# A hybrid encoder layer on one core: the residual's gate moved among the gate paths, and the rows of the first keys and queries kept in the probabilities' buffers

## The chip, the cores and the metric

The kernel runs on one core of a Trainium2 chip. The metric is the device time of one execution in microseconds (us); lower is better. The engines are TensorE (PE, matmuls; PEld are its weight loads), VectorE (DVE), ScalarE (ACT), GpSimd (POOL), and SyncE (SP), whose queue issues nearly all DMAs.

## What is computed

One encoder layer is applied to two requests (prompt and sample), each 1024 tokens of 1024 channels, with shared weights, in float32. Cut to what matters:

```python
mod = silu(c) @ w_ada + b_ada
shift, scale, gate = split(mod, 3)                 # gate: the residual's gate
h = rms_norm(x, norm_g) * (1 + scale) + shift
qa, ka, va, za, qb, kb, vb, zb, ga, gb = split(h @ w_in, ...)
qa, ka = rope_axial(rms_norm(qa, qn_a)), rope_axial(rms_norm(ka, kn_a))   # 8 and 2 heads of 64
oa = gqa_attention(qa, ka, va) * silu(za)
qb, kb = rope(rms_norm(qb, qn_b)), rope(rms_norm(kb, kn_b))               # 4 heads, two maps each
ob = rms_norm(softmax(q1 k1) v - lam * softmax(q2 k2) v, subln_g) * (1 - lam_init) * silu(zb)
merged = sigmoid(ga) * (oa @ w_proj_a) + sigmoid(gb) * (ob @ w_proj_b)
y = x + gate * (merged @ w_out)
```

## The kernel before

Everything is float32 in, float32 out. Most matmuls are split: a weight or an activation is kept as a high part (a copy in float32r, by ScalarE) and a low part (the difference, by VectorE), and a product is three matmuls. `load_w` loads 256 columns of a weight in four pieces through three small staging buffers (`st`, line 229), splits each piece (lines 203, 204) and puts the parts into one of two weight buffers (`wpool`, tag `w`, 16 KB per partition). These two buffers are shared by all weights.

The kernel is written as Python generators. Each `yield` is a step, and `weave` (line 80) draws steps from several streams in turns: each stream has a number of steps that it is thought to have and a lead, and the one that is least far along goes next. So the order in which instructions are written down comes from constants at the top of the file. A planner then fixes the order of each engine's queue at build time, from modelled durations, with the written order as priority; the attention's instructions get a higher one (line 976). On the chip every queue, TensorE's and SP's among them, runs in its fixed order and waits where it must.

One request goes like this.

- **Head** (`head`, line 1114): keys and values of branch A (`kva_gen`) and the first half of its queries (`qa_gen`). `pipelined` makes a tile of 128 tokens by `proj_tt` (a product of 24 matmuls, line 596), then a *front* (copy, squares and their sum, a power for the inverse norm, rotation: `rows`, lines 604 to 615, and `rope`, 617 to 638; on VectorE and GpSimd by turns) that leaves a finished row tile, and up to `LAG` tiles later a *back*: one or two transpositions on TensorE (line 649) and the split into keys or queries (651, 652). A row tile is one of three buffers (`rtile`, line 175).
- For the first request, products of the first four token tiles are summed while the modulation is still being made (`sums_early`); they sit in the four banks that the scores use later (`early`). So for tiles 0 to 3 `proj_tt` has nothing to do and returns the sum given.
- **Gate paths** (`z_gen`, line 786): 12 items (`z_item`) of 256 columns for `za`, `zb`, `ga`, `gb`, each of 12 steps of 8 matmuls (line 797). The result is stored to DRAM (line 784). The stream `zs` chains the 12 items, and every phase takes some of its steps: a phase takes three times its number in `Z_SHARE` (the fourth and the fifth are heads 1 and 2; the sixth isn't used).
- **Attention** (`attention`, line 959): first branch A in two halves (phases 0 and 1), then four heads of branch B (phases 2, 3, 4 and the last). A score tile is four matmuls (824, 825), a maximum (826), an exponential (828), and, once two maps are joined (860), a transposition within blocks by VectorE (861) and four DMAs (`flip`, 866) that turn the probabilities; the values follow (886, 887 for A, 926 for B). Probabilities lie in four buffers of 128 x 1024 (`ptile`, line 160).
- Beside the phases the other projections are made: the second half of the queries in phase 0, values and queries and keys of B in phase 1 and so on.
- **Last phase** (line 1256): the last head's attention, woven with `fill()` and `gates()`. `gates` multiplies branch outputs by their gates (`gated_gen`: rows are loaded again, 1028 to 1036, and split, 1043). `fill` is: what is left of `zs`, then, for the first request, `gate_gen()`, then the merges (`merge_gen`, 1070).
- After it the rest of the merges, the output projection (`out_gen`, line 1101) and, beside it, the second request's normalised input (`ht_gen`).

`gate_gen` (line 516) makes the residual's gate for both requests: four groups of 256 columns of `w_ada`. For each group, four loads of 256 KB through the staging buffers (line 525), eight matmuls (two pieces of the profile each) that put four strips of the sum into four quarters of a bank (line 528), a copy (534), two small matmuls that add the strips (537), the bias and a factor (539, 542). It yields eight times.

Of the kernel before, what the change touches and what calls it, by code (L numbers as in the profile page):

```python
# [12 lines left out]
F32 = mybir.dt.float32  # L13
F32R = mybir.dt.float32r
AF = mybir.ActivationFunctionType
ALU = mybir.AluOpType
# [18 lines left out]


Z_SHARE = (
    (8, 19, 6, 3, 3, 3),
    (13, 12, 7, 3, 0, 6),
)  # L40
Z_HEAD = (8, 6)
Z_HEAD_A = (-0.3, -0.12)
ATT_W = (
    (0.944, 1.018, 1.232, 1.187, 1.03, 1.769),
    (1.017, 1.209, 1.063, 1.196, 0.764, 1.069),
)
IN_A = (
    (0.1, -0.05, 0.7, 0.05, 0.2, 0.15),
    (0.1, -0.05, 0.43, 0.3, 0.15, 0.55),
)  # L50
Z_A = (
    (0.25, 0.05, 0.3, -0.05, -0.1, 0.0),
    (0.05, 0.05, 0.35, 0.15, -0.3, -0.2),
)
LAST_ATT = (47, 45)
LAST_FILL = (21, 25)
GATED_A = (0.1, 0.1)
LATE_A = 1.0
QUARTER_P = 200
KV_STEPS = 12  # L60
QA_A = 0.0
FIRST_ATT = 16
FIRST_A = 0.18
Z_SPLIT = 6
TAIL = (2, 5)
TAIL_A = (1.15, 1.15)
LAG = 2
Z_FIRST = (7, 10)
Z_FIRST_A = (0.0, 0.0)

CUTS = (3, 6)

# [7 lines left out]
def weave(*streams):  # L80

    live = [[g, n, 0, ahead] for g, n, ahead in streams if n > 0]
    while live:
        s = min(live, key=lambda s: s[2] / s[1] - s[3])
        if next(s[0], None) is not None:
            s[2] += 1
        else:
            live.remove(s)


def drain(*gens):
    for g in gens:
        if g is not None:
            for _ in g:
                pass
# [13 lines left out]
def kernel(ctx: ExitStack, tc: tile.TileContext, t: dict):  # L109
# [19 lines left out]
    def nm(s):  # L129
        uid[0] += 1  # L130
        return f"{s}_{uid[0]}"
# [8 lines left out]
    def gbank():  # L140
        turn[0] += 1
        if alone[0] and not early and turn[0] % 5 in (0, 2):
            return sbank()[:, :512]
        return fbank()
# [24 lines left out]
    def halves2(pt):  # L169
        return pt[:, :512], pt[:, 512:]  # L170
# [4 lines left out]
    def rtile():  # L175
        return mtile("row", [P, 512], bufs=3)
# [337 lines left out]


    def gate_gen():
        for n in range(4):
            acc = gbank()[:, :256]
            nc.vector.memset(acc, 0.0)
            for q in range(2):  # L520
                sts = []
                for i in range(2):
                    st = spool.tile([P, 2, 256], F32, tag="st", name=nm("st"))
                    row, col = q * 512 + i * 256, 2 * D + n * 256
                    dma(st, w_ada[row : row + 256, col : col + 256].rearrange("(c p) n -> p c n", p=P))
                    sts.append(st)
                for c in (2, 3, 0, 1):
                    nc.tensor.matmul(
                        acc[32 * c : 32 * c + 2], cT[:, q * 4 + c], sts[c // 2][:, c % 2], start=(q == 0), stop=(q == 1),
                        tile_position=(0, 32 * c),  # L530
                    )
                yield 1
            part = rtile()[:, :256]
            nc.vector.tensor_copy(part, acc)
            ps = gbank()[:, :4].rearrange("p (c g) -> p c g", g=2)
            for c in range(2):
                nc.tensor.matmul(ps[:, c, :], part[:, c * P : (c + 1) * P], two, start=True, stop=True)
            cs = slice(n * 2, n * 2 + 2)
            nc.vector.tensor_tensor(
                out=gatec[:, cs], in0=ps, in1=bcol[:, 2, cs].unsqueeze(2).to_broadcast([P, 2, 2]), op=ALU.add  # L540
            )
            nc.vector.tensor_scalar(out=gatec[:, cs], in0=gatec[:, cs], scalar1=0.5, scalar2=None, op0=ALU.mult)

    def ht_gen(g, ht):
        ss = const.tile([P, NTT], F32, name="ssx")
# [54 lines left out]
    def by_turns(tt):  # L600

        return nc.vector if alone[0] and tt % 2 == 0 else nc.gpsimd

    def rows(ps, nh, rs):

        n = nh * HD
        row = rtile()
        raw, sq = row[:, :n], row[:, 256 : 256 + n]
        nc.scalar.activation(raw, ps, AF.Copy)
        nc.scalar.activation(sq, raw, AF.Square, scale=1.0 / math.sqrt(HD))  # L610
        ss = tiny.tile([P, 4], F32, tag="ss", name=nm("ss"))[:, :nh]
        nc.vector.tensor_reduce(out=ss, in_=sq.rearrange("p (h d) -> p h d", d=HD), axis=AX.X, op=ALU.add)
        nc.vector.tensor_scalar(out=ss, in0=ss, scalar1=EPS, scalar2=None, op0=ALU.add)
        nc.gpsimd.tensor_tensor(out=rs, in0=ss, in1=nhalf[:, :nh], op=ALU.pow)
        return (x.rearrange("p (h d) -> p h d", d=HD) for x in (raw, sq))
# [38 lines left out]
    def pipelined(ht, w, front, back, given={}, rest=0):  # L654
        pend = []
        for tt in range(NTT):
            ps = yield from proj_tt(ht, w, tt, given)
            pend.append((tt, front(tt, ps)))
            if len(pend) > LAG:
                back(*pend.pop(0))  # L660
            if tt + 1 == rest:
                while pend:
                    back(*pend.pop(0))
            yield 1
        while pend:
            for _ in range(1 if alone[0] else 3):
                yield 1
            back(*pend.pop(0))
        yield 1
# [444 lines left out]
    def head(g, st, zs, late):  # L1114
        kva, qa = kva_gen(st["ht"], st), qa_gen(st, 0)

        def folded():
            by_q(st["cosA"], st["sinA"], gqa, 16)
            st["turned"] = True

        nz = 3 * Z_HEAD[g]
        if g == 0:
            rs = late[0]()
            weave((islice(zs, 6), 6, 0.0), (late[1](rs), 4, LATE_A))
            weave((kva, 27, 0.0), (islice(zs, Z_FIRST[0]), Z_FIRST[0], Z_FIRST_A[0]))
            drain(islice(qa, KV_STEPS))
            early.clear()
            folded()
        else:
            weave((kva, 27, 0.0), (islice(zs, Z_SPLIT), Z_SPLIT, Z_HEAD_A[0]))  # L1130
            folded()
            weave((qa, 27, 0.0), (islice(zs, nz - Z_SPLIT), nz - Z_SPLIT, Z_HEAD_A[1]))
        return qa

    def new_state(g):
# [55 lines left out]
    def z_item(st, i):  # L1191
        ht = st["ht"]
        if i < 2:
            w = kva_w[2][0] if i == 0 and st is states[0] else None
            return z_gen(ht, C_ZA + i * 256, st["zd"], i * 2, True, w)
        if i < 4:
            return z_gen(ht, C_ZB + (i - 2) * 256, st["zd"], i * 2, True)
        i -= 4
        if i % 2 == 0:
            return z_gen(ht, C_GA + i * 128, st["gad"], i, False)  # L1200
        return z_gen(ht, C_GB + (i - 1) * 128, st["gbd"], i - 1, False)
# [4 lines left out]
    for g in range(2):  # L1206
        st = states[g]
        ht = st["ht"]
        load_tables_A(st)
        zs = chain(*[z_item(st, i) for i in range(12)])  # L1210
        qa = head(g, st, zs, late)
        alone[0] = False
        if g == 0:
# [32 lines left out]

        def fill():
            yield from zs
            if g == 0:
                yield from gate_gen()  # L1250
            drain(first)
            yield from islice(merge, 16 - TAIL[g])

# [64 lines left out]
```

## Time and profile before

| | |
|---|---|
| runs | 1953.32, 1954.51, 1960.04 us; median 1954.51 |
| the profiled execution | 1953.03 us, span 1951.2 us, mean granted clock 0.982 |
| TensorE busy | 1865.0 us (96%) |
| weight loads (PEld) | 1609.4 us (82%) |
| VectorE busy | 1398.9 us (72%) |
| ScalarE, GpSimd busy | 994.9 us (51%), 412.1 us (21%) |
| DMA | 299.48 MB, mean 153 GB/s |

A row of waits reads "engine, tile, line, waited for engine, tile, line: us in total, times, longest". A row of a time line reads "start, duration, engine, line, operation, output <- input, shapes, count [idle before it <- what ended the idle]". A row of windows gives a stretch, its length, the busy time of PE, PEld, DVE, ACT and POOL with their counts of instructions, the mean granted TensorE clock, the share of the DMA engines' time and GB/s. SPq is SyncE's queue. The last attention phase of the first request runs from about 755 to 860 us; its first merge (line 1070) starts at 838.56 us.

### The profile page before, as it was taken

How to read it: one execution, taken by the hardware profiler on the slowest of the kernel's cores; microseconds unless marked ns; L12 is line 12 of the kernel's file. 1: busy time of each engine (PE TensorE's matmuls, PEld its weight loads, DVE VectorE, ACT ScalarE, POOL GpSimd, SP SyncE). 2: the span in 40 equal slices, each digit the busy share in tenths (PEclk: the TensorE clock that was granted, in tenths of full speed). 3: DMA queues.
4: the chain of work that ended last, by engine and by line, in shares of the span. 5: the costliest groups of instructions: out<-in, count | busy, mean ns of one | idle time of the engine just before them, and what ended most of it. 6: DMA issues, size and time to landing. Idle time of an engine off the chain costs nothing.

```text
span 1951.2 us, 30752 instructions
## 1 busy us (share of the span) xinstructions
PE 1865.0 (96%) x10406; PEld 1609.4 (82%) x10406; DVE 1398.9 (72%) x2160; ACT 994.9 (51%) x2095; POOL 412.1 (21%) x766
## 2 busy tenths in 40 slices
PE   6879999999999999699999999999999999999999
PEld 4768888888888898477889888888888899778887
DVE  4667986778887667767475688767878876887731
ACT  3546765666665545422333466656667555643310
POOL 0252310032424233000023322001322332410000
PEclk9989999999999999799999999999999999999999
DMA  9125555556554435887552355656565443578632
GB/s 322 47 70 149 150 158 140 156 146 153 153 145 120 104 96 141 251 281 216 200 182 63 107 133 139 186 130 169 143 160 148 129 131 99 129 239 260 216 103 76
DMA packets 280316, 299.48 MB, mean 153 GB/s; under 512 B 38304, under 2 KB 233056, under 8 KB 280160
## 3 DMA queue, kind: packets, MB, share of 16 engines
q1 hardware_dynamic: 280160, 297.51, 54.1%
q8 instruction: 84, 1.38, 0.3%
q14 instruction: 72, 0.59, 0.1%
HBM read 137.91 MB, written 42.04 MB: 92 GB/s over the span
## 4 chain that ended last, share of the span: by engine, by line
PE 58%; DVE 14%; DMA 11%; SPq 7%; issue 4%; ACT 4%; POOL 2%; ACTq 0%; DVEq 0%; POOLq 0%
PE f L596 13%; PE f L797 12%; PE f L1070 6%; DMA q<-p 6%; PE f L1101 6%; SPq L866 5%; PE a L926 4%; PE s L1101 3%; PE s L824 3%; PE s L825 3%; DVE m L826 3%; DVE q L875 3%; DVE p L861 2%; PE s L1070 2%; ACT p L828 1%
## 5 line engine op out<-in xcount | busy, mean ns | idle before, releaser
L797 PE MATMUL f<-u,w 128*128 128x512 f32 x2136 | 547.1, 394 | 4.5 <-DVE w L204 2.3
L596 PE MATMUL f<-w,u 128*128 128x256 f32 x3264 | 456.0, 285 | 0.7 <-DVE u L652 0.5
L797 PEld LDWEIGHTS f<-u,w 128*128 128x128 f32 x2136 | 387.8, 188 | 79.7 <-DVE w L204 3.5
L596 PEld LDWEIGHTS f<-w,u 128*128 128x128 f32 x3264 | 428.9, 191 | 18.2 <-DVE u L652 0.9
L826 DVE TENSOR_REDUCE m<-s 128x1 f32<-128x1024 f32 x256 | 310.9, 1218 | 42.5 <-PE s L825 39.5
L861 DVE STREAM_TRANSPOSE p<-p 128x1024 f32<-128x1024 f32 x192 | 238.3, 1241 | 105.0 <-ACT p L828 103.7
L825 PE MATMUL s<-u,sw 128*128 128x512 f32 x512 | 207.0, 405 | 0.9 <-DMA sw<-u 0.9
L875 DVE TENSOR_TENSOR q<-q,hi 128x512 fp32r<-128x512 f32 x256 | 173.0, 692 | 37.5 <-ACT hi L874 34.7
L828 ACT ACTIVATE p<-s,m,rsA 128x1024 f32<-128x1024 f32 x128 | 154.0, 1203 | 86.9 <-DMA q<-p 79.4
L874 ACT ACTIVATE hi<-q 128x512 fp32r<-128x512 f32 x256 | 152.9, 624 | 74.5 <-DMA q<-p 40.0
L828 ACT ACTIVATE p<-s,m,rsB 128x1024 f32<-128x1024 f32 x128 | 154.4, 1206 | 14.8 <-DMA q<-p 7.2
L203 ACT ACTIVATE w<-st 128x512 fp32r<-128x512 f32 x188 | 109.3, 625 | 99.2 <-PE f L1101 34.3
L204 DVE TENSOR_TENSOR w<-st,w 128x512 fp32r<-128x512 f32 x188 | 126.3, 703 | 32.9 <-ACT w L203 32.2
L1070 PE MATMUL f<-u,w 128*128 128x512 f32 x576 | 140.0, 395 | 0.6 <-DVE u L1043 0.5
L886 PE MATMUL a<-hi,u 128*128 128x256 f32 x512 | 133.0, 285 | 3.9 <-DVE oo L903 3.3
L887 PE MATMUL a<-q,u 128*128 128x256 f32 x512 | 131.0, 288 | 2.2 <-DVE q L875 2.2
L926 PE MATMUL a<-q,u 128*128 128x256 f32 x512 | 125.2, 386 | 4.9 <-DVE w L204 2.5
L1070 PEld LDWEIGHTS f<-u,w 128*128 128x128 f32 x576 | 108.7, 190 | 24.8 <-DVE u L1043 0.9
L742 POOL TENSOR_TENSOR row<-row,gB 128x96 f32<-128x96 f32 x64 | 30.0, 470 | 445.2 <-ACT row L610 445.2
L824 PE MATMUL s<-u 128*128 128x512 f32 x256 | 111.8, 437 | 9.6 <-ACT p L828 9.6
L825 PEld LDWEIGHTS s<-u,sw 128*128 128x128 f32 x512 | 99.5, 194 | 17.6 <-issue 1.1
L926 PEld LDWEIGHTS a<-q,u 128*128 128x128 f32 x512 | 96.1, 194 | 21.8 <-issue 5.6
(184 smaller groups left out, 2623.5 us busy)
## 6 DMA issues: line engine op xcount, KB each, us to landing
q<-p SPq DMA_DIRECT2D x768, 128.0 KB, 2.7
st<-in_w_in_dram SPq DMA_DIRECT2D x128, 256.0 KB, 3.2
zd<-ev SPq DMA_DIRECT2D x96, 256.0 KB, 2.2
sw<-u SPq DMA_DIRECT2D x256, 64.0 KB, 2.1
p<-zd SPq DMA_DIRECT2D x64, 256.0 KB, 3.6
u<-in_w_ada_dram SPq DMA_DIRECT2D x16, 512.0 KB, 8.8
st<-in_w_in_dram SPq DMA_DIRECT2D x64, 128.0 KB, 3.1
st<-in_w_out_dram SPq DMA_DIRECT2D x32, 256.0 KB, 3.9
```

What stands on the lines that cost most here:

```text
L596: nc.tensor.matmul(ps, lt[c][:, sl], w[c][:, wi, :], start=(k == 0), stop=(k == 23))
L797: nc.tensor.matmul(ps, w[c][:, wi, e * P : (e + 1) * P], rt[c], start=(k == 0), stop=(k == 23),)
L824: nc.tensor.matmul(s[:, sl], q, k[:, sl], start=True, stop=False)
L825: nc.tensor.matmul(s[:, sl], sw, k[:, sl], start=False, stop=True)
L826: nc.vector.tensor_reduce(out=m, in_=s, axis=AX.X, op=ALU.max, negate=True)
L828: nc.scalar.activation(pt.rearrange("p (j c a) -> p j c a", j=4, c=8), s.rearrange("p (c a j) -> p j c a", c=8, j=4), AF.Exp, scale=rs, bi ...
L861: nc.vector.transpose(pt, pt)
L874: nc.scalar.activation(th, tl.bitcast(F32), AF.Copy)
L875: nc.vector.tensor_tensor(out=tl, in0=tl.bitcast(F32), in1=th.bitcast(F32), op=ALU.subtract)
L926: nc.tensor.matmul(acc, u["v"][:, k], pT[:, k], start=(k == 0), stop=(k == 7))
L1070: nc.tensor.matmul(ps, w[:, c, wi, d * P : (d + 1) * P], o[:, oi, :], start=(k == 0), stop=(k == 11))
L1101: nc.tensor.matmul(ps, w[c][:, wi, e * P : (e + 1) * P], m[:, mi, :], start=(k == 0), stop=(k == 23))
```

## The change

- `gate_gen` no longer runs in `fill` between the last gate path and the merges. It stands in the chain `zs` of the first request behind item 9 (`GATE_AT`), as eight steps among the gate paths' steps.
- It loads 512 columns of `w_ada` at a time, in four DMAs of 512 KB, into one of the two weight buffers, twice; the staging buffers aren't used. The matmuls are the same in number and shape.
- In the first request's head the fronts of the four given tiles of keys, and then those of queries, are written down first (12 steps each), with their row tiles in halves of the probabilities' buffers (`row_early`). `pipelined` does no back while tiles are given, and yields once before the queries' four backs. Then come the rest of the keys, woven with 9 steps of the gate paths (7 before), and the queries' backs.
- In the second request's head keys and queries are one stream, woven with 18 steps of the gate paths that start later.
- Constants: steps per phase, leads, the rates of the attention in the phases, the rates in the last phase.

```diff
@@ -35,38 +35,37 @@
 
 
 Z_SHARE = (
-    (8, 19, 6, 3, 3, 3),
+    (8, 21, 4, 2, 4, 3),
     (13, 12, 7, 3, 0, 6),
 )
 Z_HEAD = (8, 6)
-Z_HEAD_A = (-0.3, -0.12)
+Z_HEAD_A = (-0.3, -0.32)
 ATT_W = (
-    (0.944, 1.018, 1.232, 1.187, 1.03, 1.769),
-    (1.017, 1.209, 1.063, 1.196, 0.764, 1.069),
+    (0.944, 1.067, 1.232, 1.093, 1.03, 1.769),
+    (1.017, 1.367, 1.063, 1.196, 0.764, 1.069),
 )
 IN_A = (
-    (0.1, -0.05, 0.7, 0.05, 0.2, 0.15),
+    (0.1, -0.07, 0.7, 0.05, 0.25, 0.15),
     (0.1, -0.05, 0.43, 0.3, 0.15, 0.55),
 )
 Z_A = (
-    (0.25, 0.05, 0.3, -0.05, -0.1, 0.0),
-    (0.05, 0.05, 0.35, 0.15, -0.3, -0.2),
+    (0.25, 0.05, 0.2, -0.05, -0.1, 0.0),
+    (0.03, 0.05, 0.35, 0.15, -0.3, -0.2),
 )
-LAST_ATT = (47, 45)
-LAST_FILL = (21, 25)
+LAST_ATT = (47, 43)
+LAST_FILL = (22, 23)
 GATED_A = (0.1, 0.1)
 LATE_A = 1.0
 QUARTER_P = 200
 KV_STEPS = 12
-QA_A = 0.0
-FIRST_ATT = 16
-FIRST_A = 0.18
-Z_SPLIT = 6
+GATE_AT = 9
+FIRST_ATT = 15
+FIRST_A = 0.16
 TAIL = (2, 5)
 TAIL_A = (1.15, 1.15)
 LAG = 2
-Z_FIRST = (7, 10)
-Z_FIRST_A = (0.0, 0.0)
+Z_FIRST = (9, 8)
+Z_FIRST_A = (-0.05, 0.0)
 
 CUTS = (3, 6)
 
@@ -514,32 +513,35 @@
 
 
     def gate_gen():
-        for n in range(4):
-            acc = gbank()[:, :256]
-            nc.vector.memset(acc, 0.0)
-            for q in range(2):
-                sts = []
-                for i in range(2):
-                    st = spool.tile([P, 2, 256], F32, tag="st", name=nm("st"))
-                    row, col = q * 512 + i * 256, 2 * D + n * 256
-                    dma(st, w_ada[row : row + 256, col : col + 256].rearrange("(c p) n -> p c n", p=P))
-                    sts.append(st)
-                for c in (2, 3, 0, 1):
-                    nc.tensor.matmul(
-                        acc[32 * c : 32 * c + 2], cT[:, q * 4 + c], sts[c // 2][:, c % 2], start=(q == 0), stop=(q == 1),
-                        tile_position=(0, 32 * c),
-                    )
-                yield 1
-            part = rtile()[:, :256]
-            nc.vector.tensor_copy(part, acc)
-            ps = gbank()[:, :4].rearrange("p (c g) -> p c g", g=2)
-            for c in range(2):
-                nc.tensor.matmul(ps[:, c, :], part[:, c * P : (c + 1) * P], two, start=True, stop=True)
-            cs = slice(n * 2, n * 2 + 2)
-            nc.vector.tensor_tensor(
-                out=gatec[:, cs], in0=ps, in1=bcol[:, 2, cs].unsqueeze(2).to_broadcast([P, 2, 2]), op=ALU.add
-            )
-            nc.vector.tensor_scalar(out=gatec[:, cs], in0=gatec[:, cs], scalar1=0.5, scalar2=None, op0=ALU.mult)
+        for half in range(2):
+            w = wpool.tile([P, NCH, 512], F32, tag="w", name=nm("wg"))
+            for q in range(4):
+                row, col = q * 256, 2 * D + half * 512
+                dma(
+                    w[:, q * 2 : q * 2 + 2],
+                    w_ada[row : row + 256, col : col + 512].rearrange("(c p) n -> p c n", p=P),
+                )
+            for n in (half * 2, half * 2 + 1):
+                cols = slice(n % 2 * 256, n % 2 * 256 + 256)
+                acc = gbank()[:, :256]
+                nc.vector.memset(acc, 0.0)
+                for q in range(2):
+                    for c in range(4):
+                        nc.tensor.matmul(
+                            acc[32 * c : 32 * c + 2], cT[:, q * 4 + c], w[:, q * 4 + c, cols], start=(q == 0),
+                            stop=(q == 1), tile_position=(0, 32 * c),
+                        )
+                    yield 1
+                part = rtile()[:, :256]
+                nc.vector.tensor_copy(part, acc)
+                ps = gbank()[:, :4].rearrange("p (c g) -> p c g", g=2)
+                for c in range(2):
+                    nc.tensor.matmul(ps[:, c, :], part[:, c * P : (c + 1) * P], two, start=True, stop=True)
+                cs = slice(n * 2, n * 2 + 2)
+                nc.vector.tensor_tensor(
+                    out=gatec[:, cs], in0=ps, in1=bcol[:, 2, cs].unsqueeze(2).to_broadcast([P, 2, 2]), op=ALU.add
+                )
+                nc.vector.tensor_scalar(out=gatec[:, cs], in0=gatec[:, cs], scalar1=0.5, scalar2=None, op0=ALU.mult)
 
     def ht_gen(g, ht):
         ss = const.tile([P, NTT], F32, name="ssx")
@@ -601,10 +603,17 @@
 
         return nc.vector if alone[0] and tt % 2 == 0 else nc.gpsimd
 
+    spare, held = [], [False]
+
+    def row_early():
+        if not spare:
+            spare.extend(halves2(ptile()))
+        return spare.pop(0)
+
     def rows(ps, nh, rs):
 
         n = nh * HD
-        row = rtile()
+        row = row_early() if held[0] else rtile()
         raw, sq = row[:, :n], row[:, 256 : 256 + n]
         nc.scalar.activation(raw, ps, AF.Copy)
         nc.scalar.activation(sq, raw, AF.Square, scale=1.0 / math.sqrt(HD))
@@ -656,9 +665,10 @@
         for tt in range(NTT):
             ps = yield from proj_tt(ht, w, tt, given)
             pend.append((tt, front(tt, ps)))
-            if len(pend) > LAG:
+            while len(pend) > LAG and tt >= len(given):
                 back(*pend.pop(0))
             if tt + 1 == rest:
+                yield 1
                 while pend:
                     back(*pend.pop(0))
             yield 1
@@ -1117,19 +1127,21 @@
         def folded():
             by_q(st["cosA"], st["sinA"], gqa, 16)
             st["turned"] = True
+            yield from ()
 
         nz = 3 * Z_HEAD[g]
         if g == 0:
             rs = late[0]()
             weave((islice(zs, 6), 6, 0.0), (late[1](rs), 4, LATE_A))
-            weave((kva, 27, 0.0), (islice(zs, Z_FIRST[0]), Z_FIRST[0], Z_FIRST_A[0]))
-            drain(islice(qa, KV_STEPS))
+            held[0] = True
+            drain(islice(kva, 12), islice(qa, 12))
+            held[0] = False
+            weave((kva, 15, 0.0), (islice(zs, Z_FIRST[0]), Z_FIRST[0], Z_FIRST_A[0]))
+            next(qa)
             early.clear()
-            folded()
+            drain(folded())
         else:
-            weave((kva, 27, 0.0), (islice(zs, Z_SPLIT), Z_SPLIT, Z_HEAD_A[0]))
-            folded()
-            weave((qa, 27, 0.0), (islice(zs, nz - Z_SPLIT), nz - Z_SPLIT, Z_HEAD_A[1]))
+            weave((chain(kva, folded(), qa), 52, 0.0), (islice(zs, nz), nz, Z_HEAD_A[g]))
         return qa
 
     def new_state(g):
@@ -1207,7 +1219,7 @@
         st = states[g]
         ht = st["ht"]
         load_tables_A(st)
-        zs = chain(*[z_item(st, i) for i in range(12)])
+        zs = chain(*[x for i in range(12) for x in (z_item(st, i), gate_gen())[: 1 + (i == GATE_AT and g == 0)]])
         qa = head(g, st, zs, late)
         alone[0] = False
         if g == 0:
@@ -1246,8 +1258,6 @@
 
         def fill():
             yield from zs
-            if g == 0:
-                yield from gate_gen()
             drain(first)
             yield from islice(merge, 16 - TAIL[g])
```

## The prediction

> **What bounds the kernel now.** First the page: the shares of the engines and the slices.
>
> ```profile
> span 1951.2 us, 30752 instructions
> PE 1865.0 (96%) x10406; PEld 1609.4 (82%) x10406; DVE 1398.9 (72%) x2160; ACT 994.9 (51%) x2095; POOL 412.1 (21%) x766
> PE   6879999999999999699999999999999999999999
> PEclk9989999999999999799999999999999999999999
> ```
>
> TensorE is the bound: 86.2 us of the span without a matmul (1951.2 - 1865.0). A schedule change can win only those and the time in which the granted clock was below 1. Both lie in two places, the first three slices and the one slice with a 6 and a 7 (the 17th). The windows, cut at the joints of the program, show how much each place holds (PE, PEld, DVE, ACT, POOL busy; clock; DMA share; GB/s):
>
> ```profile
> 60.00:105.00 45.00, 41.91 (x240) 37.33 (x239) 27.58 (x75) 20.71 (x53) 13.04 (x27) 0.92 0.13 42
> 105.00:132.00 27.00, 14.59 (x51) 9.38 (x50) 21.78 (x63) 9.71 (x29) 13.94 (x23) 0.75 0.30 71
> 132.00:755.00 623.00, 613.80 (x3658) 544.30 (x3658) 476.47 (x677) 378.33 (x802) 168.37 (x315) 1.00 0.52 136
> 755.00:778.60 23.60, 23.60 (x111) 19.58 (x110) 16.70 (x25) 11.43 (x24) 2.10 (x4) 1.00 0.64 185
> 778.60:838.60 60.00, 39.68 (x183) 25.92 (x182) 47.12 (x71) 22.62 (x44) 3.87 (x8) 0.77 0.85 254
> 838.60:1020.00 181.40, 180.66 (x797) 148.28 (x798) 113.63 (x178) 54.77 (x96) 16.09 (x15) 0.99 0.66 219
> 1020.00:1951.20 931.20, 911.83 (x5110) 794.57 (x5108) 664.74 (x1017) 472.13 (x1005) 192.77 (x369) 0.99 0.52 145
> ```
>
> Place A, 105 to 132 us: 12.4 us idle, and 14.59 busy at clock 0.75, which at full clock would be 10.9: 3.7 more. Together 16.1. Place B, 778.6 to 838.6: 20.3 idle and 39.68 at 0.77, so 9.1 more. Together 29.4. All else is nearly full: 9.2 idle in 132 to 755, 19.4 in the whole second request.
>
> Who made TensorE wait in place B, and in place A (views of the waits, window 740 to 870, then 105 to 132):
>
> ```profile
> PE f L528 <- DMA st<-in_w_ada_dram: 11.9, 4, 4.6
> PE s L824 <- ACT p L828: 4.6, 3, 3.9
> PE f L537 <- DVE row L534: 3.5, 2, 2.9
> ```
>
> ```profile
> PE f L649 <- DVE row L638: 5.0, 1, 5.0
> PE f L649 <- POOL row L638: 3.3, 2, 2.3
> PE f L797 <- DVE w L204: 1.4, 2, 1.2
> PE s L824 <- DVE u L652: 1.3, 1, 1.3
> PE f L797 <- ACT w L203: 0.7, 1, 0.7
> PE s L825 <- DMA sw<-u: 0.7, 1, 0.7
> ```
>
> L528 and L537 are the residual's gate: 15.4 of the 20 us, its matmuls stand in TensorE's queue before the next scores. L649 is the transposition of a finished row: 8.3 of A's 12.4.
>
> **The change, part by part.**
>
> Steps of the gate paths ("z steps", 8 matmuls each), counted from the constants. Before: 23 in the head, 24, 57, 18, 9, 9 in the five phases, 4 left for the last one, then 8 gate steps. After: 23, 24, 63, 12, 6, 12, and 12 left; the gate's 8 steps are the 121st to the 128th, the end of the phase of head 0 and all of the phase of head 1. So the last phase gets 12 z steps where it had 4 and 8 of the gate; the phases of heads 0 and 1 lose 17 z steps and get 8 of the gate. Prices, from the time lines:
>
> ```profile
> 166.14 5.60 PE L797 MATMUL f<-u,w 128*128 128x512 f32 x24
> 811.10 0.61 PE L528 MATMUL f<-st,cT 128*2 128x256 f32 x8
> 814.38 0.50 PE L537 MATMUL f<-two,row 128*128 128x2 f32 x4
> 60.83 0.69 DVE L204 TENSOR_TENSOR u<-st,u 128x512 fp32r<-128x512 f32 x1
> 767.69 0.27 DVE L519 MEMSET f<- 128x256 f32 x1 [0.42 <-ACT ev L779]
> 801.30 0.41 DVE L534 COPY row<-f 128x256 f32<-128x256 f32 x1
> ```
>
> A z step is 5.60/3 = 1.87 us, the gate 8 x 0.61 + 4 x 0.50 = 6.9 us of TensorE, and on VectorE 4 x (0.27 + 0.41 and two tiny operations, about 0.3) = 4.0 us. Its 16 loads of 256 KB become 8 of 512 KB, the same 4 MB.
>
> *Last phase.* The stretch 755 to 838.6 (83.6 us) gives up the gate and takes eight z steps, 15.0 us. TensorE's need at full clock becomes 23.6 + 39.68 x 0.77 - 6.9 + 15.0 = 62.3 us. VectorE's becomes 16.70 + 47.12 - 4.0 + 2.8 (four splits of 0.69 for the weights of the item that now falls here) = 62.6 us. Below 62.6 the stretch can't go; if the stalls are replaced by others of the same size it stays at 83.6. How full VectorE can run beside TensorE I take from two other stretches, and from the one that the change thins out (540 to 722):
>
> ```profile
> 200.00:250.00 50.00, 50.00 (x299) 44.35 (x298) 48.72 (x68) 36.20 (x79) 15.38 (x21) 1.00 0.56 143
> 540.00:722.00 182.00, 178.12 (x1073) 159.00 (x1072) 131.68 (x190) 99.62 (x215) 60.38 (x122) 1.00 0.45 118
> 1450.00:1500.00 50.00, 46.09 (x267) 39.71 (x266) 40.64 (x61) 33.70 (x72) 13.23 (x30) 0.97 0.56 138
> ```
>
> It reached 97% with no gap on TensorE (200 to 250), while in the whole of 132 to 755 it is 76%. I take the middle, 87%: 62.6/0.87 = 72 us. The stretch saves 83.6 - 72 = 11.6 (between 21.0 and 0). The earlier phases lose 15.0 of z work and get the gate's 6.9: 8.1 saved, since TensorE is full there. **Sum for the last phase: -19.7** (ends -29.1 and -8.1). What is late next there is the scores' wait for the probabilities (L824 on L828, 4.6 us now), which is the same attention chain, paced by VectorE's maxima and transposes.
>
> *The thinner phases.* 540 to 722 holds most of heads 0 and 1. It loses 17 x 1.87 = 31.8 us of TensorE and gets 6.9: 178.1 becomes 153, against a VectorE need that stays near 131.7 (the gate's 4.0 comes, 17/12 of a weight split of 2.8 goes). That is 86% where it was 72%. The row of 1450 to 1500, with VectorE at 81%, had 3.9 us of gap in 50, which would be 12 us on 153; the row of 200 to 250 had none at 97%. The stretch had 3.9 of gap itself. I take **+3** (0 to +12), nearer to the second row since projections of queries, keys and values stay as cover.
>
> *Gate weights in whole buffers.* They no longer pass through the small staging buffers, so the projection weights of branch A aren't queued behind them there (each stood in SP's queue after L525). But their DMAs can't be issued before one of the two weight buffers is free, that is until the last matmul of an earlier item. Rows for a load of that size, and for SP's present waits on weight loads:
>
> ```profile
> u<-in_w_ada_dram SPq DMA_DIRECT2D x16, 512.0 KB, 8.8
> SPq L234 <- DVE w L204: 95.8, 56, 15.0
> ```
>
> Behind a waiting SP stand the turns of the probabilities (L866), the swapped queries (L678) and the stores of z; the scores wait for them in turn. Two halves are loaded, each at most 8.8 us late at TensorE: 0 to 17.6. The four present waits are 11.9/4 = 3.0 each. I take one of them, **+3**, since the other engines' projections can stand ahead of the gate in TensorE's order.
>
> The Trainium skill ("DMA: Bandwidth & Descriptors", section "Anatomy of one DMA — SWDGE (gpsimd) path") says that a DMA's semaphore wait is held on the issuing sequencer before dispatch. The row of SP's waits agrees: 95.8 us in 56 waits, one of them 15.0.
>
> *Head.* The four early tiles of keys and of queries get rows in halves of the four probability buffers, so all eight fronts (square, sums, rotation) are emitted before the rest of the keys; before, three row buffers let the queries' fronts run only at 108 to 131, mixed with the last keys. Nothing is added: the same instructions move ahead. Their cover is the row 60 to 105, with VectorE free for 45 - 27.58 = 17 us and GpSimd for 32; in 105 to 132 VectorE is busy 21.8 of 27. Two of the rows that show the tangle, and one of the constants' loads in VectorE's order:
>
> ```profile
> 113.09 0.43 POOL L698 TENSOR_TENSOR row<-row,rs 128x128 f32<-128x128 f32 x1
> 122.13 0.66 PE L649 MATMUL f<-ident,row 128*128 128x128 f32 x2 [4.95 <-DVE row L638]
> 119.06 0.29 DVE L498 TENSOR_TENSOR p<-p 128x128 f32<-128x128 f32 x1 [2.20 <-DMA p<-in_lam_k_dram]
> ```
>
> The last key tile waits for GpSimd at 113, behind powers for query rows; the first query row waits behind the constants. With the fronts done, the 8.3 us of L649 should go. The 4.1 of the other rows of place A (2.1 for z weights, 1.3 and 0.7 for transposed queries and their swap) stay, and with them half of the clock's 3.7: 16.1 - 5.9 = 10.2. Off goes 2 for keys delayed while the late half of h fills VectorE, and for lambda's buffer, which now has to wait until key rows leave a probability buffer. **-8** (ends -16 and +2: the z steps that the head gains, 9 and 8 for 7 and 10, are the same 17).
>
> *Constants, second request.* Its queries follow its keys in one stream, z steps come later in it; the last phase's rates move a little. Its gaps are 19.4 us in 931, scattered. **0** (-6 to +6, a third of those gaps).
>
> Sum: 1953.0 (the profiled run's own time: span 1951.2 and 1.8 around it; the median of the runs is 1954.5) - 19.7 + 3 + 3 - 8 + 0 = **1931.3**. I say 1931.
>
> **The rivals.**
>
> *The last phase is VectorE's chain anyway.* The stalls at L528 only hid that scores wait for maxima, exponentials and flips. Then z work fills the gaps, and the stretch keeps its 83.6 us: the gain there is 8.1, total 1931.3 + 11.6 = 1943. For it: VectorE 47.12 of 60 busy even with the stalls. Against: the row of 200 to 250.
>
> *The clock comes back whole.* The rows of long gaps in place B, and one of the matmuls after a short one in A:
>
> ```profile
> 784.22 0.79 PE L824 MATMUL s<-u 128*128 128x512 f32 x1 [3.87 <-ACT p L828]
> 799.95 1.03 PE L528 MATMUL f<-st,cT 128*2 128x256 f32 x8 [4.62 <-DMA st<-in_w_ada_dram]
> 818.45 1.03 PE L528 MATMUL f<-st,cT 128*2 128x256 f32 x8 [3.56 <-DMA st<-in_w_ada_dram]
> 126.34 0.80 PE L824 MATMUL s<-u,u 128*128 128x512 f32 x1 [1.30 <-DVE u L652]
> ```
>
> After gaps of 3.6 to 4.6 us a step of the gate took 1.03 instead of 0.61. If only such long ones cost clock and none is left, the stretch ends near TensorE's own need, at about 64, and the total is 1931.3 - 8 = 1923. The last row, slow after 1.30, speaks against, though 4.95 stood shortly before it. The Trainium skill ("TensorE: Matmul & The Clock Gate", section "Why this matters for your kernels") has such a rule: gaps over about 3 us between bursts drop the clock, shorter ones don't. By that rule the total would be that of this rival; the first three rows agree, the fourth leaves it open.
>
> *Nothing much.* The head gains nothing (its rows collide with the late half of h), the last phase its 8.1, and the thinner phases and the loads take 6 of it: 1951, no change to be told.
>
> *Slower: SP stands still for the gate's weights.* Place: between the ninth and the eleventh gate path, where both halves wait for a buffer that an item holds (12 steps, 22 us). SP waits 15 us (its longest now) twice, no flip is issued, and the projections meant as cover have no weights either, since their loads stand in the same queue: 30 us in all, 1961. It decides from about 22 us of uncovered standstill on, which would eat the whole gain. Against: the order is planned with these waits known, and most of SP's 56 are short (95.8/56 = 1.7).
>
> **How the numbers follow.** Chances: forecast (1924 to 1939) 0.46, clock back whole (1923) 0.15, VectorE's chain (1943) 0.18, nothing much (1951) 0.11, standstill (1961) 0.10. The three gains hold 0.79: faster by over 0.3% (5.9 us, about the spread of the three runs, 1953.32 to 1960.04). Same 0.11, slower 0.10. The range goes to 1916 (the last phase at TensorE's need and the head at its better end, half of each) and to 1949, which leaves out the last two rivals.
>
> **What would show it.** Right: no TensorE wait on w_ada after the start, the gate's matmuls between about 600 and 710 us, z matmuls (L797) within the last attention phase until just before the first merge, clock 0.95 or more there, and the first merge some 22 us earlier than 838.6 (8 from the head, 20 from the gate, 6 given back). In the head, L649 waits under 2 us and the first scores near 116 instead of 124. Wrong: a long SP wait on the gate's loads, gaps over 10 us between 540 and 700 with scores waiting for L828, or new waits for rows around 84 to 105.

## The result, and the profile after

| kernel | median us | ratio to before, 95% interval |
|---|---|---|
| before | 1957.28 (1953.32 to 1962.1) | |
| changed | 1940.31 (1938.53 to 1942.49) | 0.9913 [0.9884, 0.9941] |
| changed, timed again | 1940.66, before beside it 1961.35 | 0.9892 [0.9872, 0.9913] |

The change makes the kernel about 1% faster: 17 us by the first comparison, 21 by the second. Forecast were 1931 us and a gain of about 22 us. The page of the changed kernel (its profiled execution took 1940.72 us):

```profile
span 1938.9 us, 30718 instructions
PE 1858.5 (96%) x10406; PEld 1606.0 (83%) x10406; DVE 1393.9 (72%) x2160; ACT 994.9 (51%) x2095; POOL 414.0 (21%) x766
PE   6899999999999999999999999999999999998999
PEclk9899999999999999999999999999999999999999
```

The 6 and the 7 of the 17th slice are gone. But of the 12.3 us by which the span is shorter only 5.8 are gaps (86.2 became 80.4); 6.5 is less busy time for the same 10406 matmuls, at a mean granted clock of 0.991 instead of 0.982. To compare the kernels stage by stage I cut both at the same events: the first score of the last head, and the first matmul of the first request's output projection. The first two rows are before, the next three the changed kernel (the first of them is the head's place A):

```profile
754.70:934.30 179.60, 158.54 (x709) 123.06 (x708) 131.16 (x206) 63.86 (x119) 9.96 (x18) 0.91 0.76 234
934.30:1951.20 1016.90, 997.53 (x5492) 865.59 (x5490) 711.33 (x1084) 497.10 (x1051) 204.99 (x378) 0.99 0.53 150
```

```profile
105.00:132.00 27.00, 23.89 (x121) 18.54 (x120) 18.49 (x52) 10.46 (x30) 8.68 (x16) 0.94 0.33 78
754.10:913.60 159.50, 149.64 (x666) 121.74 (x665) 123.14 (x183) 61.13 (x117) 11.12 (x17) 1.00 0.78 235
913.60:1938.90 1025.30, 998.22 (x5492) 865.24 (x5490) 710.23 (x1084) 496.75 (x1051) 207.47 (x378) 1.00 0.52 149
```

The stretch of the last phase and the merges of the first request is 20.1 us shorter, its gap falls from 21.1 to 9.9 us, and its clock rises from 0.91 to 1.00. It begins at about the same time (754.1 and 754.7). Ahead of it TensorE does 61 gate-path matmuls fewer (some 7.6 steps), but all of the gate and 16 matmuls of the values more, and it is busy for 710.7 us instead of 709.0. So the earlier phases give next to nothing to the gain. The second request is 8.4 us longer in this pair of profiles.

Where the changed kernel's TensorE waits now in that stretch (view of the waits), and the gate's weights (from the view of that tile; the last line is the gate's matmul of before, from the view of its line):

```profile
PE f L1024 <- POOL ssB L966: 3.1, 1, 3.1
PE f L1080 <- ACT u L1052: 1.9, 1, 1.9
PE f L1080 <- DVE ssB L960: 1.9, 1, 1.9
PE a L936 <- DMA q<-p: 1.2, 1, 1.2
PE a L936 <- DMA row<-zd: 0.9, 1, 0.9
PE f L1080 <- DVE u L1053: 0.8, 1, 0.8
```

```profile
L530 PEld LDWEIGHTS f<-wg,cT x64: 80/83/85, 579.1 to 673.0; 128*2 128x2 f32 x64
L530 PE MATMUL f<-wg,cT x64: 377/378/379, 579.1 to 673.2; 128*2 128x256 f32 x64
L520 SPq DMA_DIRECT2D wg<-in_w_ada_dram x8: 368/468/1711, 547.3 to 602.0; - x8
its engine sat idle before it (us, times) until:
  issue: 1.6, 5
who waited for it (us, times):
  ACT w L202: 0.6, 1
```

```profile
L528 PE MATMUL f<-st,cT x64: 377/482/634, 778.6 to 834.7; 128*2 128x256 f32 x64
```

No matmul waits for w_ada there any more. The gate's DMAs were issued from 547 us on. Its matmuls ran from 579 to 673 us (forecast was about 600 to 710) and took 377 to 379 ns each, where the median was 482. Of the 9.8 us of waits left, 7.7 are for the last head's finished rows: their norms (L960, L966) and their split (L1052, L1053).

### The profile page after: what moved, and what is told of

Same layout as the page of the kernel before. It is cut to its first block, busy times and chain, and to the rows that moved or that the text cites. A ratio compares the mean times of both kernels' runs of the same rounds, so it can differ in the third digit from the quotient of the medians.

```text
span 1938.9 us, 30718 instructions
## 1 busy us (share of the span) xinstructions
PE 1858.5 (96%) x10406; PEld 1606.0 (83%) x10406; DVE 1393.9 (72%) x2160; ACT 994.9 (51%) x2095; POOL 414.0 (21%) x766
## 4 chain that ended last, share of the span: by engine, by line
PE 53%; DVE 16%; DMA 12%; ACT 6%; SPq 5%; issue 5%; POOL 2%; ACTq 0%; DVEq 0%; POOLq 0%
PE f L807 12%; PE f L598 12%; DMA q<-p 6%; PE f L1111 6%; PE f L1080 4%; DVE m L836 4%; SPq L876 4%; PE s L1111 3%; DVE p L871 3%; PE a L936 3%; PE s L834 3%; PE s L835 3%; DVE q L885 2%; ACT p L838 2%; PE s L1080 2%
## 5 line engine op out<-in xcount | busy, mean ns | idle before, releaser
L807 PE MATMUL f<-u,w 128*128 128x512 f32 x2184 | 560.0, 394 | 5.1 <-DVE w L203 1.8
L807 PEld LDWEIGHTS f<-u,w 128*128 128x128 f32 x2184 | 394.9, 188 | 81.5 <-DVE w L203 3.1
L1080 PE MATMUL f<-u,w 128*128 128x512 f32 x576 | 139.1, 393 | 4.7 <-ACT u L1052 1.9
L1080 PEld LDWEIGHTS f<-u,w 128*128 128x128 f32 x576 | 107.4, 188 | 29.3 <-ACT u L1052 2.3
```

What stands on the lines that cost most here:

```text
L807: nc.tensor.matmul(ps, w[c][:, wi, e * P : (e + 1) * P], rt[c], start=(k == 0), stop=(k == 23),)
L1080: nc.tensor.matmul(ps, w[:, c, wi, d * P : (d + 1) * P], o[:, oi, :], start=(k == 0), stop=(k == 11))
```

## The experiments

**1. Each half of the change alone, and the gate left out.** `gate_alone` is the kernel before with the new `gate_gen` in the chain of gate paths and the first request's steps of the changed kernel; `head_alone` is the kernel before with the new head alone. `no_gate` leaves the gate's computation out of the kernel before:

```diff
-            if g == 0:
-                yield from gate_gen()
+            if g == 0:
+                nc.vector.memset(gatec, 0.5)
```

> The kernel before with the gate's part alone (whole weight buffers, item behind gate path 9, the first request's steps, leads and rates of the changed kernel); the head and the second request as before. Theory (the gate's move is worth about 15 us, the head about 6, and the second request gives about 8 back): the output projection of the first request starts some 15 us earlier than 934.3, at about 919, and as the second request is untouched the whole gain stays: 1938 to 1940 us in its profiled run, ratio to before about 0.992. Rival (the second request loses whatever comes before it, since its phases shift against the DMAs): output projection at 919, but only 7 us of gain at the end, ratio 0.996.

> The kernel before with the head's part alone (rows of the given tiles in the probabilities' buffers, order of the head, its steps); the gate and the second request as before. Theory: -5 to -6 us by the first phase of branch B and the same at the end, ratio about 0.997. Rival (the gain seen up to branch B comes from other leads in the phases, not from the head): within 2 us of before, ratio 0.999 to 1.0. The wait for a key row on VectorE (4.9 us in the changed kernel) should be there again in either case.

> The kernel before without the residual's gate: no loads of it, no matmuls, its columns set to a constant (that part of the computation is left out). It tells what the waits at the gate cost by themselves, without other work in their place. Theory of the prediction (the last phase is then near VectorE's need, 62.6 less nothing, at about 72 us instead of 83.6): about -12 us, 1941 us, ratio 0.994. Rival (the gate's waits set the whole gap): -20 of gap, -9 of clock and -7 of its own work, up to 30 us less, ratio 0.985. Rival (attention's chain sets it anyway): -3 us or less, gaps at the scores instead, ratio 0.998.

Measured: gate alone 0.9919 [0.9903, 0.9935], head alone 1.0054 [1.0038, 1.0069], no gate 1.0009 [0.9996, 1.0021]. The gate's part carries most of the gain. Its stretch from the last head's first score to the output projection has 12.0 us of gap (the profile is of its fastest run, 1937.99 us, where the median is 1945.28):

```profile
751.10:918.70 167.60, 155.61 (x683) 125.66 (x682) 125.39 (x189) 63.02 (x121) 9.91 (x17) 0.99 0.76 230
```

The head's part by itself makes the kernel slower, by 10 us; neither theory had that. And the kernel without the gate is no faster. The same stretch of that kernel, and its longest waits there:

```profile
754.70:928.30 173.60, 151.93 (x628) 120.90 (x627) 126.35 (x190) 59.20 (x114) 11.04 (x22) 0.92 0.71 214
```

```profile
PE s L824 <- ACT p L828: 6.0, 3, 4.1
PE a L926 <- DMA q<-p: 5.1, 2, 2.5
PE f L1014 <- POOL ssB L956: 2.3, 1, 2.3
PE s L1070 <- DVE u L1081: 2.2, 1, 2.2
PE f L1070 <- ACT u L1042: 2.1, 2, 1.4
PE f L1070 <- DVE u L1081: 1.9, 1, 1.9
```

The gap is 173.6 - 151.9 = 21.7 us, as with the gate (21.1). The waits of L528 and L537 are gone, and the same time is now spent waiting for probabilities, their turns and finished rows. In this profile the stretch is shorter by 6 us, about the gate's own work. So the rival that the waits only hid other waits is right for this gap: it keeps its size under other names. The timed runs show no gain at all. Part of that lies elsewhere: the second request of this profile takes 1030.3 us, 9.5 and 13.4 us more than in two profiles of before, and why was not looked into.

**2. The fill without the gate's move.** `z_late`: the kernel before, gate in its old place, but 13 gate-path steps left for the last phase instead of 4. The number of steps that `fill` is thought to have (`LAST_FILL`) goes up with them; that constant was not tried alone.

```diff
-    (8, 19, 6, 3, 3, 3),
+    (8, 21, 3, 0, 4, 3),
-LAST_FILL = (21, 25)
+LAST_FILL = (28, 25)
```

> The kernel before with 13 steps of the gate paths left for the last phase instead of 4 (taken from the phases of heads 0 and 1), and the gate still behind them in its old place, through its old buffers. Theory (the gap of the last phase is the attention's own pace, and steps of the gate paths are what fills it): nearly the whole gain of the gate's move, -10 to -15 us, ratio 0.993 to 0.995, though the gate's loads are still waited for. Rival (the gate's loads must be out of the last phase): the fill comes ahead of the stalls and the stalls stay, -3 us or less, ratio 0.998 or more.

Measured: 1.0061 [1.0041, 1.0081], slower by 12 us. Windows from the first score of head 0 to that of the last head and on to the output projection; and the longest wait:

```profile
520.10:747.90 227.80, 216.82 (x1309) 193.11 (x1310) 176.71 (x264) 132.21 (x293) 87.48 (x188) 0.98 0.45 113
747.90:947.30 199.40, 171.86 (x770) 135.02 (x769) 128.56 (x200) 63.19 (x118) 7.46 (x16) 0.91 0.70 213
```

```profile
PE f L528 <- DMA st<-in_w_ada_dram: 15.5, 4, 4.5
```

The fill was done by 794 us, ahead of the gate. Then the gate's stalls came all the same (gap 27.5 us in the stretch, which grew by 19.8 us), and the phases of heads 0 to 2, which gave up steps, have 11.0 us of gap where before has 3.9 (236.8 less 232.9 busy). The theory that fill alone is what counts falls. In these runs a gain came only with both: gate-path steps in the last phase, and the gate out of it. All seven kernels here with the gate moved have ratios between 0.988 and 0.995, all four others between 0.999 and 1.006.

**3. Whole buffers or staging, new place or old.** `gate_staged` is the changed kernel with the old body of `gate_gen` (256 KB pieces through the staging buffers) at the new place. `gate_in_place` is the kernel before with the new body (whole buffers) at the old place.

> The changed kernel with the gate at its new place, but loaded in pieces of 256 KB through the three staging buffers as before. Theory (what counts is which work fills the last phase, not the buffers): within 3 us of the changed kernel, ratio 0.991 to 0.993. Rival (the whole buffers are what takes the stalls away): waits of TensorE on these loads come back in the phases of heads 0 and 1, 8 to 12 us, ratio 0.996.

> The kernel before with the gate in its old place and all steps as before, but loaded into whole weight buffers (512 KB pieces, no staging). Theory (two conditions: the gate's waits must go, and gate-path steps must take their place; leaving the gate out altogether changed nothing): the waits on w_ada shrink under 5 us, the gap of the last phase stays near 20 us at the scores and merges, ratio 0.997 to 1.002. Rival (whole buffers are the main thing, since the staged version of the move lost half of the gain): ratio 0.992 to 0.995.

Measured: staged at the new place 0.9946 [0.9927, 0.9965], against 0.9892 for the changed kernel in the same comparison: 0.5%, half of the gain, goes with the buffers at this place. Whole buffers at the old place: 0.9988 [0.9974, 1.0001], no difference that can be told. The stretch of head 2 in the staged kernel, from its first score to that of the last head, then the same of the changed kernel:

```profile
644.30:756.50 112.20, 103.38 (x660) 91.37 (x660) 66.84 (x109) 49.47 (x110) 32.85 (x68) 0.94 0.40 106
```

```profile
652.70:754.10 101.40, 100.67 (x652) 91.18 (x652) 65.86 (x105) 50.38 (x111) 32.38 (x68) 1.00 0.42 110
```

The staged kernel has 8.8 us of gap and a clock of 0.94 here, against 0.7 and 1.00. L527 waits 2.9 us for w_ada, and scores 3.4 for probabilities. It enters this stretch 8.4 us ahead and leaves it 2.4 behind; its last stretch is then longer by 5.6 (165.1 and 159.5), with 37 matmuls more in it. Each new kernel also gets a new order from the planner, and how much of the 0.5% is that and how much the buffers was not separated. At the old place the whole buffers do away with the waits on w_ada (no row of them is left after the head), but the gap stays, 21.5 us of 180.2, like that without the gate; 6.4 us of it still stand at the gate's own lines, waiting for VectorE.

**4. The second request's constants, and the order in the last phase.** `r2_as_before` is the changed kernel with the second request's constants and head as before; it is also `gate_alone` plus the head. Four lines of its edit:

```diff
-LAST_ATT = (47, 43)
-LAST_FILL = (22, 23)
+LAST_ATT = (47, 45)
+LAST_FILL = (22, 25)
```

Two more kernels start from it, with the first request's last fill at 20 and at 24 instead of 22. The changed kernel and the one before were also profiled a second time.

> The changed kernel with all constants and the head of the second request as before. Theory (the constants cost 8 us): the same up to the output projection of the first request (913.6), and the second request takes its 1012 to 1013 us of before again instead of 1021: about 1932 us, ratio to before about 0.987. Rival (not the constants, but the shift of the planner's order by what comes before): stays at 1938 to 1942, ratio 0.991.

> The changed kernel with the second request as before, and the last phase's fill of the first request at 20 instead of 22 (attention further ahead of the merges). Theory (what gap is left, some 7 to 10 us, lies between merges and the last head's late values): the waits of merges on the last rows shrink, -3 us against the same kernel with 22, ratio to before about 0.985 to 0.987. Rival (attention can't go faster than VectorE and the turns' DMAs): the gaps move ahead of the first merge, ratio 0.988 to 0.990.

> The changed kernel with the second request as before, and the last phase's fill of the first request at 24 instead of 22, that is, gate-path steps and merges further ahead of the attention; at 20 it lost 0.7%. Theory (attention should trail: its units then find VectorE free beside merges): as 22 or up to 3 us better, ratio 0.987 to 0.989. Rival (22 is at the joint of two losses): merges run out before the last head's rows are there, gap of 5 us more ahead of the output projection, ratio 0.991 to 0.993.

> The changed kernel itself, timed beside the others of this call, and a second profile of it. Theory (the second request of the changed kernel is longer by its constants): again about 1025 us from the first output-projection matmul of the first request to the end, 1940 us, ratio 0.991. Rival (profiles of single runs differ by some 8 us in the second request whatever the constants): its length comes out near 1017 to 1020.

> The kernel before once more, for a second profile. Theory (the first profile was one of the fast executions, and lengths of the second request scatter by some 8 us): 1955 to 1962 us, the second request 1018 to 1028 us from its first profile's 1017. Rival (the second request of before takes 1017 each time, and the changed one's 1025 are its constants): within 2 us of 1017.

Measured: 0.9883 [0.9867, 0.9899] with the second request as before, and 0.9951 [0.9931, 0.9970] and 0.9890 [0.9868, 0.9912] with fills of 20 and 24. So 20 loses 0.7%, and 22 and 24 can't be told apart. The second run of before took 1961.73 us under the profiler. The second request, from the output projection to the end, took 1025.4 us in the second profile of the changed kernel (1025.3 in the first). With the constants of before it took 1016.9 and 1020.8 (before, twice), 1017.5 (gate alone), 1020.4, 1024.8 and 1024.7 (the three of this part), 1021.4 (gate in place), 1022.1 (`z_late`), 1022.0 (experiment 5), 1027.2 (head alone) and 1030.3 (no gate). The changed constants stand within a scatter of 13 us, and the intervals of the timed ratios overlap (0.9892 and 0.9883). That they cost 8 us, as the first pair of profiles looked like, is not shown; a cost of 0 to 5 us is possible.

What the head's part does beside the gate's is shown better, by two kernels of one comparison: 0.9919 [0.9903, 0.9935] without it, 0.9883 [0.9867, 0.9899] with it. It gains 0.4%, where alone it lost 0.5%. In the profiles the gain is not made in the head: with it the last head's first score comes at 755.7 us, without it at 751.1. It shows in the stretch behind, with 7.3 us of gap instead of 12.0 and 17 matmuls fewer to do (one profile of each, that of gate alone being its fastest run):

```profile
755.70:914.40 158.70, 151.38 (x666) 122.63 (x665) 123.46 (x183) 61.02 (x117) 12.17 (x17) 0.99 0.77 237
```

**5. The queries' fronts among the keys instead of ahead of them.** From `r2_as_before`:

```diff
-            drain(islice(kva, 12), islice(qa, 12))
+            drain(islice(kva, 12))
...
-            weave((kva, 15, 0.0), (islice(zs, Z_FIRST[0]), Z_FIRST[0], Z_FIRST_A[0]))
+            weave((kva, 15, 0.0), (islice(zs, Z_FIRST[0]), Z_FIRST[0], Z_FIRST_A[0]), (queries(), 12, -0.2))
```

> The changed kernel with the second request as before, and in the head the fronts of the early query tiles written down among the remaining keys (12 steps beside 15, a fifth behind) instead of ahead of them. Theory (the 4.9 us for which the transposition of a key row waits for VectorE come from query rotations ahead of it): that wait falls under 2 us and the first score comes 2 to 4 us earlier than 121 to 123; ratio 0.986 to 0.988. Rival (the wait only moves to the queries' rows behind): first score at the same time, ratio 0.988 to 0.990.

Measured: 0.9878 [0.9858, 0.9898], the same as `r2_as_before`; the first score comes at 123.8 us (121.4 there). The longest waits in the head, of the changed kernel and then of this one:

```profile
PE f L658 <- DVE p L647: 4.9, 1, 4.9
PE f L658 <- DVE u L661: 1.2, 2, 0.6
```

```profile
PE f L658 <- POOL row L647: 4.4, 1, 4.4
PE s L834 <- DVE u L661: 3.3, 2, 3.2
PE f L658 <- DVE p L647: 2.1, 1, 2.1
```

The key row's wait falls from 4.9 to 2.1 us (it is 5.0 in `r2_as_before`) and comes back as 4.4 for a row on GpSimd: the rival. No kernel here beats the changed one by more than the intervals.

## Why the prediction came out near, by its own steps

The time lies outside the band of the forecast's own case (1924 to 1939) and nearer to the rival of VectorE's chain (1943) than to 1931. As a ratio, 0.9913 and 0.9892 stand nearer to the forecast (1931.3 / 1953.0 = 0.9889) than to that rival (1943 / 1953.0 = 0.9949), and the rival's mechanism, a stretch that keeps its length, did not come. That the sum is so near is in part luck. Two pairs of profiles (the second one is below, before and then the changed kernel) show it, step by step. Up to the last head's first score the sum took off 10.1 us (8.1 and 8, less 3 and 3); 0.6 and 2.8 us came. From there it took off 11.6; 20.1 and 21.9 came. For the second request it took off nothing; it got longer by 8.4 and 4.6. Misses of 7 to 10 us in the first two steps cancel.

```profile
757.50:939.20 181.70, 160.63 (x708) 124.73 (x707) 131.59 (x206) 63.86 (x119) 10.00 (x18) 0.90 0.75 231
754.70:914.50 159.80, 152.42 (x666) 124.30 (x665) 122.93 (x182) 60.47 (x115) 12.13 (x17) 0.98 0.78 235
```

- **Last phase, -19.7 (with +3 and +3 for the thinner phases and the loads: -13.7).** The size is right for the gate's part: gate alone gains 0.81% of 1961, 16 us. The reason was half wrong. The prediction gave 15.4 of the 20 us of gap to the gate's waits, by the view of the waits. Without the gate the gap is as large (experiment 1): behind the wait that ended last stood others of the same size. What the price itself came from, the sum of needs, did better: with TensorE's 62.3 and VectorE's 62.6 us in a stretch of 83.6 there was room for 15 us of gate-path work, and it was used. But room alone is not enough: by the same sum `z_late` had room too (23.6 + 30.6 + 9 x 1.87 = 71 us of TensorE in 83.6), and lost. Nor was the share of 87% reached at which VectorE was to run: from the last head's first score to its last values it was busy for 80% of 99.8 us (the first two rows below), before for 74% of 116.8 (the last two).
- **The first merge 22 us earlier than 838.6.** It came at 796.4, 42 us earlier: more of the last head's attention now runs beside the merges (its values end 57.5 us after the first merge; before, 32.9). The end of the merges moved by 20.7 us.

```profile
754.10:796.40 42.30, 42.18 (x192) 34.54 (x191) 31.73 (x43) 20.15 (x42) 4.64 (x8) 1.00 0.75 218
796.40:853.90 57.50, 53.52 (x239) 43.67 (x238) 47.94 (x69) 22.30 (x45) 4.63 (x7) 1.00 0.84 256
754.70:838.60 83.90, 63.58 (x296) 45.80 (x294) 64.11 (x95) 34.05 (x68) 6.08 (x13) 0.84 0.79 233
838.60:871.50 32.90, 32.90 (x144) 27.04 (x144) 22.62 (x38) 11.12 (x19) 2.02 (x3) 0.95 0.88 294
```

- **Thinner phases, +3.** From head 0's first score to the last head's, the gaps were 230.7 - 222.3 = 8.4 us against 3.9: +4.5, inside the bounds.

```profile
523.40:754.10 230.70, 222.30 (x1389) 195.45 (x1388) 177.46 (x278) 132.66 (x289) 84.76 (x177) 0.99 0.49 131
517.90:754.70 236.80, 232.92 (x1395) 207.56 (x1394) 174.78 (x260) 133.35 (x291) 88.09 (x177) 1.00 0.45 116
```

(The first row is the changed kernel's, the second that of before.)

- **Loads into whole buffers, +3 as a loss only.** Too much: no matmul's wait on them is seen. SP's standstill, the slower rival, didn't come either: its longest wait at the line of these loads is 2.8 us. Against loads through the staging buffers at the new place the kernel is 10 us faster (0.9946 to 0.9892), at the old place it is not (experiment 3). The prediction named the staging queue but gave its relief no price.
- **Head, -8.** Beside the gate's move its part gains 0.4%, some 7 us, near the -8, but not where the prediction put it (experiment 4): the size is luck. L649's 8.3 us became 4.9 for one key row at 95 us plus small ones: "new waits for rows around 84 to 105" was named as a way to be wrong. Place A itself improved, from 12.4 us of gap to 3.1 and from clock 0.75 to 0.94, but part of it moved ahead of 105. The first score came at 122.8 us (124.2 before), not near 116. Alone the head's part costs 10 us, though not in the head: its profile is 0.8 us ahead of that of before at head 0's first score and 11.4 behind at the output projection, with 24.8 us of gap in that stretch (187.8 less 163.0 busy) and a clock of 0.88. Waits on w_ada are shorter in that stretch (8.3 us, before 11.9), and waits of scores for probabilities longer (10.8, before 4.6). Why, and why the same head gains with the gate moved, was not taken apart further.
- **Second request, 0 (-6 to +6).** +8.4 in the first pair of profiles, +3 against the mean of the eleven profiles with the constants of before; not separable from scatter.
- **Clock back whole (1923).** In the stretch 754.1 to 913.6 the clock did come back whole, to 1.00 (0.98 in the second profile); but late rows of the last head, above all, kept 9.9 us of gap, so the time didn't follow. The Trainium skill ("TensorE: Matmul & The Clock Gate", section "Why this matters for your kernels") sets the limit at gaps of about 3 us. The runs here show no sharp one. A gap of 3.1 us (L1024, above) left the clock at 1.00. In the second request of the changed kernel two shorter ones close together, 2.3 and 1.1 us, came with a clock of 0.90 (the gaps, then the windows):

```profile
1750.53 0.50 PE L834 MATMUL s<-u 128*128 128x512 f32 x1 [2.27 <-ACT p L838]
1752.86 5.16 PE L936 MATMUL a<-q,u 128*128 128x256 f32 x16 [1.14 <-DMA st<-in_w_proj_a_dram]
```

```profile
1742.50:1755.00 12.50, 9.10 (x35) 6.92 (x35) 10.34 (x16) 6.31 (x13) 0.34 (x1) 0.90 0.79 238
1755.00:1763.70 8.70, 8.70 (x38) 7.25 (x38) 5.49 (x8) 1.94 (x4) 0.00 (x0) 0.95 0.56 197
```

## What to carry to other kernels

The view of the waits names who came last, not what the wait costs. Where two engines share a stretch, add up what each must do in it, and ask what is late when the named wait is gone. Here leaving the waiting work out gained nothing, filling the stretch without moving that work lost, and moving it and filling its place gained 16 us. A step of a schedule constant (a fill of 20 for 22, 0.7%) is worth as much as a change of buffers (0.5%), and the head's part loses alone and gains beside the gate's. So the parts of such a change can't be priced one by one and added. And a sum that comes out near says little until its steps are compared one by one with two profiles.

## What the runs showed that was not expected

The same program in the same order on every queue took 1951.2 and 1960.0 us in two profiles: 4.9 us of it up to the output projection of the first request, 3.9 after it. So differences of a few us between single profiles, the second request's lengths above all, were not read as causes here; the timed ratios decide.
